# Modulation steps in the middle of wide token products, and q and k of a neighbourhood attention in 256 columns

## The chip, the cores and the metric

The kernel runs on one core of one Trainium2 chip. The metric is the time of one launch on the device in microseconds (us), the median of a few runs.

## The reference, cut to what matters

Two transformer blocks stand one behind the other, 256 tokens of x and 256 tokens of a context, 1024 features, all in float32. The first has two layers: modulation, a projection (`w_in`), differential attention, a short convolution and a Fourier mix, a projection back (`w_out`), layer norm, and an MLP of width 4096 with a squared ReLU. The second has an even layer (latent attention and a convolution) and an odd layer (RWKV with a decay, and a neighbourhood attention), each followed by 16 experts. What the change touches is this:

```python
mod_x = silu(c) @ w_mod[l] + b_mod[l]            # 6 * 1024 columns, for x and for ctx
sh1, sc1, g1, sh2, sc2, g2 = split(mod_x, 6)
px = (x * (1 + sc1) + sh1) @ w_in[l]
x = layer_norm(ALPHA * x + g1 * (mix_x @ w_out[l]))
x = layer_norm(ALPHA * x + g2 * (relu((x * (1 + sc2) + sh2) @ w_up[l]) ** 2 @ w_down[l]))
...
u = h @ od_w_in; uc = hc @ od_w_in               # odd layer: 1920 RWKV columns, then q, k, v
q, k = rms_norm(q by head), rms_norm(k by head)  # 8 heads of 64; q of x alone, k of x and ctx
```

## The kernel before

The program is laid out in the order of the blocks, and a scheduler puts each engine's instructions in a fixed order at build time: an instruction goes as early as its inputs, buffers and its rank in the program allow, by the scheduler's own estimate of times. On the chip each engine then runs its list in order. Buffers of one name are handed out in program order from a small pool: two PSUM banks "ps", two "pS", one "pt", two "pd", one "pm" (`BANKS`, L572).

**Products.** A float32 product is done as three: each operand is split into a high part (ScalarE cast, L347) and the rest (VectorE subtraction, L350), and high x high, high x low and low x high are summed in PSUM (L327 issues all of them). `by_features` (L398) takes weights of 256 columns as one load of 1 MB and gives features x tokens. `by_tokens` (L422) takes 512 columns as two loads of 1 MB, each 512 rows deep, and gives tokens x 512 columns: it opens one bank per block of 128 tokens, goes through four pairs of 128 rows, splits a pair (L383, three buffers each for the parts "wh" and "wl"), and multiplies it into every bank, so all banks are complete at the end. The banks are taken in turn from `WIDE` (L571). It is called for V (L756) and the output projection (L880) of the first block's mixer, for the second MLP matrix (L947), for the latent attention (L1186, L1200), the even layer's output (L1311) and the odd layer's q, k and v (L1693, L1698).

**The weight ring.** All loads of weights take a slot of 1 MB (`raw`, L366): three in one pool and one in another, used by every fourth load. They are issued on SyncE's queue (SP).

**Modulation steps.** Each of the four modulations (first block's layers, second block's layers) is a generator of 24 steps, eight for each of three banks of 2048 columns (`mods_steps`, L482). A step is one load of 1 MB through the ring (L532) and four small products into the bank "pm"; the eighth step of a bank copies it out (L502), transposes it through "ps" and adds the bias. `fill(n)` (L535) advances the front generator by n steps, up to a limit that the stages raise. Every call of `by_features` and of `by_tokens` ends with `fill(self.rate)`, the rate being 1. Before the output projection `need(m, 1)` (L866) and at the start of the MLP `need(m, 2)` (L902) force what is missing of a bank. Then `fill(BF[2 * l])` (L907) hands out four more, of the next modulation. In the first layer's mixer nine products come before the output projection (k twice, q twice, V, four others), and 16 steps, two banks, must be done by the MLP; in the second layer's mixer two steps come before the nine products. The second block's first modulation may hand out 18 steps (`NF`) until its own layer begins.

**The odd layer's input stage** (`odd_in`, L1628). RWKV's columns go by features. Then `lengths` (the norm of k in RWKV), the transposes of V (L1681), and `low_rank` (L1685: eight products of decays and rates) each use "ps" banks in turn. Then `NO` (L1554) lists k (tokens of x and context, four blocks), q (two blocks) and v (four blocks). k and q are copied out into tiles "nz" of two token blocks x 512 columns (two buffers), normed by head (`head_norm`, L990: per 512 columns a square into a "ps" bank by ScalarE and a sum by VectorE; then a chain of eleven small VectorE instructions for the root, and one multiplication), transposed 128 x 128 through "ps" and copied to the tiles "nk" and "nq" (L1708). The pools of the stage close after it, and the RWKV core follows.

Of the kernel before, what the change touches and what calls it, by code (L numbers as in the profile page):

```python
# [74 lines left out]
def every(n, w=256):  # L75
    return [(c, w) for c in range(0, n, w)]
# [9 lines left out]
def lay_out(inp):  # L86
# [10 lines left out]
    for name, blocks, rows in (  # L97
            ("ev_w_in_2", [(1184, 256), (672, 256), (1440, 256), (928, 256), (384, 256), (640, 32), (0, 256), (256, 128)],
             None),
            ("ev_w_out_2", every(1024, 512), 512), ("mla_w_uq_2", [(0, 512), (512, 256)], None),  # L100
            ("mla_w_ukv_2", every(1024, 512), None), ("od_w_in_2", every(1792) + [(1792, 128)], None),
            ("od_w_in_2", [(1920 + c, 512) for c in range(0, 1536, 512)], 512)):
        packs.setdefault(name, Packed())
        packs[name].add(g[name][0], blocks, rows)
    packs["od_w_out_2"] = Packed()
# [143 lines left out]
class Kernel:  # L249
# [148 lines left out]
    def by_features(self, src, ah, al, n, evac, halves=False, raw=None, le=None):  # L398
# [20 lines left out]
                self.fill(self.between)  # L419
        self.fill(self.rate)  # L420

    def by_tokens(self, srcs, ah, al, tbs, evac, ks=None):  # L422


        srcs = sorted(srcs, key=lambda z: ks.index(z[1])) if ks else srcs
        raws = [(self.load(z), k0) for z, k0 in srcs]
        ps = {tb: self.psum(self.bank()) for tb in tbs}
        pairs = [(raw, k0, i) for raw, k0 in raws for i in range(0, raw.shape[1], 2)]
        if ks:
            pairs.sort(key=lambda z: ks.index(z[1] + z[2]))  # L430
        for n, (raw, k0, i) in enumerate(pairs):
            kn, w = min(2, raw.shape[1] - i), raw.shape[2]
            wh, wl = self.parts(raw[:, i:i + kn])
            for tb in tbs:
                ts, out = slice(tb * 128, (tb + 1) * 128), ps[tb][:, :w]
                for j in range(kn):
                    h, l = ah[k0 + i + j][:, ts], al[k0 + i + j][:, ts]
                    end = n == len(pairs) - 1 and j == kn - 1
                    self.mm(out, h, wh[:, j], n + j == 0, False)
                    self.mm(out, h, wl[:, j], False, False)  # L440
                    self.mm(out, l, wh[:, j], False, end)
                if n == len(pairs) - 1:
                    evac(tb, out)
        self.fill(self.rate)

    def halves(self, w, c0, *where, first=0):
# [1125 lines left out]
class Odd(Moe):  # L1572
# [55 lines left out]
    def odd_in(self, m, od):  # L1628
# [3 lines left out]
        with self.dense():  # L1632
# [58 lines left out]
            for c0, n, dT in NO:  # L1691
                if dT is None:
# [1 line left out]
                                   lambda tb, ps: nc.scalar.copy(self.nv[:, tb], ps))  # L1694
                    continue
                dT = self.nkT if n == 4 else self.nqT
                zs = [tmp.tile([128, 2, 512], F32, name="nz", bufs=2) for _ in range(n // 2)]
                self.by_tokens(self.halves(a["od_w_in_2"], c0), ahs, als, range(n),  # L1698
                               lambda tb, ps: nc.scalar.copy(zs[tb // 2][:, tb % 2], ps))
                for tp, z in enumerate(zs):  # L1700
                    self.head_norm(z.rearrange("p t (h d) -> p (t h) d", h=8), 64)
                    for i in range(0, 4, 2):
                        ps = self.psum()
                        for i2 in range(2):
                            for tb in range(2):
                                self.transpose(ps[:, i2 * 256 + tb * 128:i2 * 256 + (tb + 1) * 128],
                                               z[:, tb, (i + i2) * 128:(i + i2 + 1) * 128])
                        nc.scalar.activation(dT[:, i:i + 2, tp * 256:(tp + 1) * 256],  # L1708
                                             ps.rearrange("p (i t) -> p i t", i=2), AF.Copy, scale=gain if n == 2 else 1.0)

    def lengths(self):

# [482 lines left out]
```

## Time and profile before

| what | value |
|---|---|
| median of three runs | 2853.8 us (2849.46 to 2855.07) |
| the profiled execution | 2856.6 us, of which its span 2854.8 us |
| TensorE (PE) busy | 2577.0 us |
| VectorE (DVE), ScalarE (ACT), GpSimd (POOL) busy | 1183.4, 770.8, 300.0 us |
| DMA over the span | 683.40 MB, mean 239 GB/s |
| first block and even layer, experts 1, odd layer, experts 2 | about 0 to 1400, 1400 to 1880, 1880 to 2390, 2390 to 2855 us |

All times within the profile are counted from the start of the span. A row of the timeline has the start, the duration, engine, line, operation, "tile written <- tiles read", shapes and count; in square brackets the engine's idle time before it and what ended that. A row of the slices of time has for each engine the busy time and, in brackets, the number of instructions. PEclk is the granted share of TensorE's full clock. Matmuls overlap, so the time of one is read from the distance of neighbours or from a run of many.

### The profile page before, as it was taken

What the parts mean: (1) busy time and instruction counts of PE and PEld (TensorE: products, weight loads), DVE (VectorE), ACT (ScalarE), POOL (GpSimd) and SP (SyncE); (2) the same over time, 40 slices, a digit from 0 to 9 for tenths busy, and PEclk for the clock granted to TensorE, in tenths of its full rate; (3) what the DMA queues carried; (4) which work ended last, traced back from release to release, by engine and by line L of the source; (5) the groups of instructions that cost most, each with busy time, mean ns of one, the idle gap of its engine ahead of it and who ended that gap; (6) DMA issues with size and microseconds to landing.
All of it is one profiled execution on the core that took longest, in us unless ns stands there. A gap on an engine that the chain in (4) does not pass through costs nothing.

```text
span 2854.8 us, 34268 instructions
## 1 busy us (share of the span) xinstructions
PE 2577.0 (90%) x13719; PEld 1563.0 (55%) x13719; DVE 1183.4 (41%) x2226; ACT 770.8 (27%) x1395; POOL 300.0 (11%) x361
## 2 busy tenths in 40 slices
PE   7998899997998998989799999989896997888888
PEld 4666688885765796757543333357544684222121
DVE  3365633346456467997401111155359362000000
ACT  3342322222333343366410000033442432000000
POOL 0001400004002003300100000000033130000000
PEclk9999999998999999999899999989898798999999
DMA  7335522223447764242599999952185558999998
GB/s 303 132 133 185 199 89 104 90 102 135 150 161 284 258 213 178 69 166 97 219 395 419 420 420 420 420 205 101 34 239 132 142 167 339 421 421 422 421 422 351
DMA packets 147215, 683.40 MB, mean 239 GB/s; under 512 B 38384, under 2 KB 51568, under 8 KB 71920
## 3 DMA queue, kind: packets, MB, share of 16 engines
q1 hardware_dynamic: 140800, 664.32, 60.6%
q10 hardware_dynamic: 6256, 16.90, 1.8%
q8 instruction: 108, 1.77, 0.3%
q14 instruction: 51, 0.42, 0.0%
HBM read 667.73 MB, written 11.60 MB: 238 GB/s over the span
## 4 chain that ended last, share of the span: by engine, by line
PE 54%; DMA 23%; DVE 8%; issue 2%; ACT 2%; POOL 0%; SPq 0%; DVEq 0%; POOLq 0%; ACTq 0%
DMA w<-in_moe_w 21%; PE pd L327 19%; PE pS L327 12%; PE pu L327 6%; PE pt L327 5%; PE ps L327 3%; PE pg L327 2%; PE pm L327 2%; DVE al L364 1%; PE pt L451 1%; PE ps L451 1%; PE pO L327 1%; DVE fs L1940 1%; PE py L327 1%; DVE co L1123 1%
## 5 line engine op out<-in xcount | busy, mean ns | idle before, releaser
L327 PE MATMUL pu<-w,xs 128*64 128x512 f32 (+1 forms) x2024 | 503.7, 599 | 41.4 <-DMA w<-in_moe_w 40.6
L350 DVE TENSOR_TENSOR wl<-w,wh 128x1024 fp32r<-128x1024 f32 x229 | 285.3, 1248 | 365.9 <-ACT wh L347 360.1
L347 ACT CAST wh<-w 128x1024 fp32r<-128x1024 f32 x250 | 259.8, 1043 | 609.9 <-PE pd L327 294.3
L327 PEld LDWEIGHTS pu<-w,xs 128*64 128x64 f32 (+1 forms) x2024 | 147.2, 123 | 374.7 <-issue 260.5
L327 PE MATMUL pd<-w,hidT 128*64 128x512 f32 (+1 forms) x1024 | 259.5, 598 | 30.3 <-DMA w<-in_moe_w 30.2
L327 PE MATMUL pd<-ah,wh 128*128 128x512 f32 (+2 forms) x656 | 233.5, 361 | 9.3 <-ACT wh L347 5.0
L327 PE MATMUL pd<-al,wh 128*128 128x512 f32 (+2 forms) x656 | 232.4, 356 | 6.7 <-DVE al L364 6.7
L327 PE MATMUL pd<-ah,wl 128*128 128x512 f32 (+1 forms) x648 | 227.5, 352 | 0.0
L1524 ACT ACTIVATE hid<-pu 128x512 f32<-128x512 f32 x24 | 14.2, 598 | 676.3 <-PE pu L327 676.3
L327 PEld LDWEIGHTS pd<-w,hidT 128*64 128x64 f32 (+1 forms) x1024 | 76.6, 122 | 198.3 <-issue 114.8
L1525 DVE TENSOR_TENSOR hid<-hid,pu 128x512 f32<-128x512 f32 x24 | 16.4, 688 | 396.9 <-PE pu L327 356.7
L327 PEld LDWEIGHTS pd<-ah,wh 128*128 128x128 f32 (+1 forms) x656 | 128.0, 197 | 46.5 <-issue 18.4
L327 PE MATMUL pm<-w,sil 128*32 128x512 f32 x640 | 108.5, 692 | 43.3 <-DMA w<-in_w_mod 31.0
L1534 DVE TENSOR_TENSOR ys<-pd,g 128x512 f32<-128x512 f32 x24 | 16.6, 692 | 315.1 <-PE pd L327 314.9
L327 PEld LDWEIGHTS pd<-al,wh 128*128 128x128 f32 (+1 forms) x656 | 128.4, 196 | 30.5 <-issue 8.3
L327 PEld LDWEIGHTS pd<-ah,wl 128*128 128x128 f32 x648 | 126.8, 196 | 20.3 <-issue 5.2
L1544 DVE TENSOR_TENSOR X<-X,ps 128x512 f32<-128x512 f32 x80 | 55.0, 688 | 128.1 <-PE ps L327 128.1
L1123 DVE SCALAR_TENSOR_TENSOR co<-cv,cols,co 128x512 f32<-128x512 f32 x120 | 100.9, 866 | 0.4
L327 PE MATMUL pS<-al,wh 128*128 128x256 f32 (+1 forms) x264 | 89.5, 340 | 4.2 <-DVE al L364 4.2
L327 PE MATMUL pS<-ah,wh 128*128 128x256 f32 (+1 forms) x264 | 89.3, 339 | 3.7 <-DVE tf L359 3.2
L327 PE MATMUL pS<-ah,wl 128*128 128x256 f32 (+1 forms) x264 | 88.6, 336 | 0.0
L327 PE MATMUL ps<-ys,gt 128*128 128x512 f32 x160 | 83.3, 629 | 0.6 <-DVE X L1544 0.6
(589 smaller groups left out, 4424.9 us busy)
## 6 DMA issues: line engine op xcount, KB each, us to landing
w<-in_moe_w SPq DMA_DIRECT2D x381, 1024.0 KB, 19.8
w<-in_w_mod SPq DMA_DIRECT2D x48, 1024.0 KB, 6.3
w<-in_w_up SPq DMA_DIRECT2D x32, 1024.0 KB, 4.8
w<-in_w_down SPq DMA_DIRECT2D x32, 1024.0 KB, 4.8
w<-in_ada_w SPq DMA_DIRECT2D x32, 1024.0 KB, 5.7
w<-in_w_in SPq DMA_DIRECT2D x20, 1024.0 KB, 4.8
mw<-in_ada_w SPq DMA_DIRECT2D x64, 256.0 KB, 3.5
w<-in_od_w_in SPq DMA_DIRECT2D x13, 1024.0 KB, 4.9
```

What stands on the lines that cost most here:

```text
L327: ins = self.nc.tensor.matmul(out, lhsT, rhs, start=start, stop=stop, skip_group_check=True)
L347: nc.scalar.copy(h, src)
L350: (le or nc.vector).tensor_tensor(l, src, h.bitcast(F32), OP.subtract)
L364: nc.vector.tensor_tensor(l, t, h.bitcast(F32), OP.subtract)
L451: ins = self.nc.tensor.transpose(out, in_, self.ident[:rows, :rows])
L1123: nc.vector.scalar_tensor_tensor(y, CV[:, f, :, t:t + T], self.col(f"dw{t}", f), y, OP.mult, OP.add)
L1524: nc.scalar.activation(hid[:, cs], up["moe_w1_2"][c], AF.Silu)
L1525: nc.vector.tensor_tensor(hid[:, cs], hid[:, cs], up["moe_w3_2"][c], OP.mult)
L1534: nc.vector.tensor_tensor(ys[:, cs], down[c], gate[:, cs], OP.mult)
L1544: nc.vector.tensor_tensor(self.X[tb][:, cs], self.X[tb][:, cs], ps, OP.add)
L1940: nc.vector.tensor_tensor(t, LM[:, s, tr, None].to_broadcast([128, nt_, nj]), X[:, s, None, jr].to_broadcast([128, nt_, nj]), OP.mult)
```

## The change

In `by_tokens` a call of `fill(self.rate)` is added after half of the pairs, where there are two or more; the one at the end stays. q and k of the neighbourhood attention are packed as four blocks of 1024 rows x 256 columns in place of two of 512 columns. A new function `by_pairs` loads such a block (1 MB), splits it in two parts, and multiplies it for two token blocks at a time into one bank, so that a bank is complete before the next is begun. The tile "nz" now holds all token blocks of 256 columns (four heads), still with two buffers, and norm, transposes and copies go by these column halves: two norms for k and two for q, where there were two for k (by token halves) and one for q. v is as before.

```diff
-("mla_w_ukv_2", every(1024, 512), None), ("od_w_in_2", every(1792) + [(1792, 128)], None),
-("od_w_in_2", [(1920 + c, 512) for c in range(0, 1536, 512)], 512)):
+("mla_w_ukv_2", every(1024, 512), None), ("od_w_in_2", every(1792) + [(1792, 128)] + [(1920 + c, 256) for c in range(0, 1024, 256)], None),
+("od_w_in_2", [(2944, 512)], 512)):
...
+    def by_pairs(self, src, ah, al, tbs, evac, ks=None):
+
+        raw = self.load(src)
+        kt, w = raw.shape[1], raw.shape[2]
+        ws = [self.parts(raw[:, k0:min(k0 + 4, kt)]) for k0 in range(0, kt, 4)]
+        for tp in tbs:
+            ps = self.psum(self.bank())
+            for i in range(2):
+                ts = slice((tp * 2 + i) * 128, (tp * 2 + i + 1) * 128)
+                out = ps[:, i * w:(i + 1) * w]
+                for n, k in enumerate(ks or range(kt)):
+                    h, l = ah[k][:, ts], al[k][:, ts]
+                    wh, wl = (z[:, k % 4] for z in ws[k // 4])
+                    self.mm(out, h, wh, n == 0 and i == 0, False)
+                    self.mm(out, h, wl, False, False)
+                    self.mm(out, l, wh, False, n == kt - 1)
+            evac(tp, ps[:, :2 * w].rearrange("p (a b) -> p a b", a=2))
+        self.fill(self.rate)
+
...
                 if n == len(pairs) - 1:
                     evac(tb, out)
+            if n == len(pairs) // 2 - 1:
+                self.fill(self.rate)
         self.fill(self.rate)
...
-                zs = [tmp.tile([128, 2, 512], F32, name="nz", bufs=2) for _ in range(n // 2)]
-                self.by_tokens(self.halves(a["od_w_in_2"], c0), ahs, als, range(n),
-                               lambda tb, ps: nc.scalar.copy(zs[tb // 2][:, tb % 2], ps))
-                for tp, z in enumerate(zs):
-                    self.head_norm(z.rearrange("p t (h d) -> p (t h) d", h=8), 64)
-                    for i in range(0, 4, 2):
+                for j in range(2):
+                    z = tmp.tile([128, 4, 256], F32, name="nz", bufs=2)[:, :n]
+                    self.by_pairs(W(c0 + j * 256), ahs, als, range(n // 2),
+                                   lambda tp, ps: nc.scalar.copy(z[:, tp * 2:tp * 2 + 2], ps))
+                    self.head_norm(z.rearrange("p t (h d) -> p (t h) d", h=4), 64)
+                    for i in range(2):
                         ps = self.psum()
-                        for i2 in range(2):
-                            for tb in range(2):
-                                self.transpose(ps[:, i2 * 256 + tb * 128:i2 * 256 + (tb + 1) * 128],
-                                               z[:, tb, (i + i2) * 128:(i + i2 + 1) * 128])
-                        nc.scalar.activation(dT[:, i:i + 2, tp * 256:(tp + 1) * 256],
-                                             ps.rearrange("p (i t) -> p i t", i=2), AF.Copy, scale=gain if n == 2 else 1.0)
+                        for tb in range(n):
+                            self.transpose(ps[:, tb * 128:(tb + 1) * 128], z[:, tb, i * 128:(i + 1) * 128])
+                        nc.scalar.activation(dT[:, 2 * j + i], ps[:, :n * 128], AF.Copy, scale=gain if n == 2 else 1.0)
```

## Rows read from the trace of the kernel before

**Rows 1.** The page: busy time, the chain that ended last, step loads (us to landing).
```profile
PE 2577.0 (90%) x13719; PEld 1563.0 (55%) x13719; DVE 1183.4 (41%) x2226; ACT 770.8 (27%) x1395; POOL 300.0 (11%) x361
...
PE 54%; DMA 23%; DVE 8%; issue 2%; ACT 2%; POOL 0%; SPq 0%; DVEq 0%; POOLq 0%; ACTq 0%
...
w<-in_w_mod SPq DMA_DIRECT2D x48, 1024.0 KB, 6.3
```

**Rows 2.** Slices of 10 us in the first layer's mixer.
```profile
220.00:230.00 10.00, 10.00 (x68) 8.99 (x67) 4.51 (x16) 3.27 (x7) 1.82 (x4) 1.00 0.00 0
...
250.00:260.00 10.00, 4.82 (x26) 1.43 (x28) 2.09 (x4) 0.00 (x0) 0.00 (x0) 0.84 0.89 360
```

**Rows 3.** Timeline of TensorE, first layer's output product.
```profile
252.17 1.07 PE L327 MATMUL pm<-w,sil 128*32 128x512 f32 x8 [0.96 <-DMA w<-in_w_mod]
257.46 3.22 PE L327 MATMUL pm<-w,sil 128*32 128x512 f32 x16 [4.22 <-DMA w<-in_w_mod]
```

**Rows 4.** Timeline of TensorE, second layer, ahead of the output product.
```profile
823.70 1.11 PE L451 MATMUL ps<-cst,tf 128*128 128x128 f32 x4 [4.38 <-DVE tf L794]
```

**Rows 5.** Timeline of TensorE, second layer's output product and start of the MLP.
```profile
850.82 1.06 PE L327 MATMUL pm<-w,sil 128*32 128x512 f32 x6
...
857.03 2.77 PE L327 MATMUL pm<-w,sil 128*32 128x512 f32 x20
...
862.11 1.07 PE L327 MATMUL pm<-w,sil 128*32 128x512 f32 x8 [0.97 <-ACT sil L490]
...
871.78 0.39 PE L327 MATMUL pt<-ah,wh 128*128 128x256 f32 x1 [1.19 <-ACT wh L347]
...
879.31 0.58 PE L327 MATMUL pt<-ah,wl 128*128 128x256 f32 x1 [7.03 <-DVE wl L350]
```

**Rows 6.** Timeline of SP's queue there.
```profile
863.24 0.33 SPq L380 DMA_DIRECT2D w<-in_w_up  x1
```

**Rows 7.** Timelines of VectorE and GpSimd there.
```profile
869.98 0.76 DVE L364 TENSOR_TENSOR al<-tf,ah 128x256 fp32r<-128x256 f32 x2
...
870.77 2.45 DVE L364 TENSOR_TENSOR al<-tf,ah 128x256 fp32r<-128x256 f32 x1
...
876.35 2.90 DVE L350 TENSOR_TENSOR wl<-w,wh 128x1024 fp32r<-128x1024 f32 x1
...
870.57 4.86 POOL L625 TENSOR_TENSOR X<-X,gb 128x1024 f32<-128x1024 f32 x2 [4.99 <-PE ps L451]
875.39 6.09 POOL L626 TENSOR_TENSOR X<-X,gb 128x1024 f32<-128x1024 f32 x2
```

**Rows 8.** Chain that ended last, odd layer's input stage (start, us, what, count).
```profile
1953.25 5.44 PE pS L327 x24
...
1964.44 2.88 PE pS L327 x24
...
2047.26 6.64 PE pS L327 x18
```

**Rows 9.** Slice of 10 us at the end of the odd layer's input stage.
```profile
2035.00:2045.00 10.00, 3.83 (x14) 2.16 (x13) 4.53 (x14) 2.51 (x5) 0.00 (x0) 0.84 0.00 0
```

**Rows 10.** Timelines of ScalarE, TensorE and VectorE in that stage.
```profile
2003.64 0.59 ACT L1699 COPY nz<-pd 128x512 f32<-128x512 f32 x1 [0.77 <-PE pd L327]
...
2035.71 1.98 PE L327 MATMUL ps<-lwa,low 64*128 64x512 f32 x4
2043.86 1.94 PE L451 MATMUL ps<-cst,nz 128*128 128x128 f32 x8 [6.17 <-DVE nz L1003]
...
2057.61 1.03 PE L451 MATMUL ps<-cst,nz 128*128 128x128 f32 x8
...
2059.22 0.61 ACT L999 ACTIVATE ps<-nz 128x512 f32<-128x512 f32 x1
...
2063.89 1.22 DVE L1003 TENSOR_TENSOR nz<-nz,rstd 128x1024 f32<-128x1024 f32 x1
...
2067.24 0.69 ACT L1708 ACTIVATE nq<-ps,nag 128x512 f32<-128x512 f32 x1 [0.17 <-PE ps L451]
```

## The prediction

> **What bounds the kernel now.** I read the page first: TensorE is busy 90% of the span, and the chain that ended last is 54% TensorE and 23% DMA [rows 1]. So the kernel is a TensorE chain with one DMA stretch in it (the expert weights), and a change pays where TensorE sits idle, or where an instruction that blocks its in-order queue goes. I then looked at the two places that the diff touches, in slices of 10 us and instruction by instruction.
>
> The first place is the modulation steps. A step is one load of 1 MB and four small products, 1.06 us of TensorE [rows 5]. In the first mixer the DMA engines moved nothing from 220 to 230 us, and from 250 to 260 TensorE was busy for less than half while they ran at 0.89 [rows 2]. What TensorE waited for there were step loads: 0.96 and 4.22 us, and the two steps behind the second wait took 3.22 us [rows 3]. The loads come in a burst because a ring of four slots holds all weights, and the steps that nobody handed out earlier are forced at the end of the mixer, behind the four loads of the output product.
>
> The same holds in the second layer, with another price. Its forced steps run until 859.8, the next modulation's first step runs at 862.11, and only when that has given its slot back, at 863.2, is the first load of the MLP issued, at 863.24 [rows 5, 6]. TensorE then waits 1.19 us for the high part of that load's split and 7.03 us for its low part [rows 5], which VectorE does at 876.35 in 2.90 us [rows 7], while GpSimd runs.
>
> The second place is the last part of the RWKV/neighbourhood input stage. TensorE is full until 2037.7; in the next ten microseconds it is busy for 3.83 [rows 9]. From there to 2067.9 the head norms of k (two) and q (one) follow each other, since all of them, and before them the decay and rate products, take the two "ps" banks in program order. The core of the RWKV part starts when the last copy is out [rows 10].
>
> **The change part by part.** (1) *Steps handed out in the middle of wide products.* Counting in the code: in the first layer V now hands out two steps and each of the two output products two, so two steps are forced where five were; in the second layer none where three were. The total of steps, of their loads on SP's queue and of their TensorE time is the same, so the gain is only in waits.
>
> First layer: at most the two waits, 5.2 us, and the slow part of 3.22 against two steps at 1.06, 1.1 us: 6.3 us. One of the forced steps keeps a slot that the last half of the output weights gives back late; a step load takes 6.3 us to land at the median [rows 1], and it is placed on TensorE's queue as now. I leave 2.3 us of waiting to it and take **-4**; bounds 0 and -6.3.
>
> Second layer: two steps inside the output product, of 1.06 us like the one at 850.82 [rows 5], can run earlier, in the idle 4.38 us before 823.70 [rows 4]: -2.1, bounds 0 and -2.1. Then the MLP's first load: its slot no longer waits for forced steps, so the split can be done before GpSimd's pass begins at 870.57 [rows 7]. That takes away 1.19 us [rows 5], and from VectorE's queue one split of 2.90 us; what is late next are the low parts "al", of which one took 2.45 us in that stretch and two together 0.76 us just before [rows 7]. By rows -4.1, bounds 0 and -8.2 (both waits whole).
>
> The Trainium skill has a rule against this: in "SBUF — State Buffer", section "Who interferes with whom", a VectorE instruction with two SBUF inputs and a GpSimd instruction that reads SBUF exclude each other, and the later one waits for the end of the other. The trace agrees in kind (2.45 us against 0.38). By that rule alone the last "al" would still come at the end of GpSimd's work, and the term would be about -1.3.
>
> GpSimd's passes stay where they are and last to 881.5 or so, so some of the low parts remain slow; I take **-3** for the load and **-2** for the two steps.
>
> New in both mixers is that the second output product's loads follow the release of the first's in the ring, where some followed a step's: they have half a product, 5 us and more, against a landing of about that [rows 1], and behind them on SP's queue stand step loads only. Late, they would hold a split on ScalarE and the products behind it: 0, bounds 0 and +2.
>
> In the second layer's MLP the 18 allowed steps go out earlier by a few products; TensorE is full there and the DMA engines are not, so 0, and if a load came late its wait would stand there (about 1 us each). In the other calls of the token products the limits stop every step, or the product is a single pair: 0.
>
> (2) *k and q by 256 columns.* Product time: 144 products of 512 columns become 288 of 256. 24 of the first kind take 5.44 us and 24 of the second 2.88 [rows 8], 0.227 and 0.120 us each: 288 x 0.120 - 144 x 0.227 = **+1.9 us**, on a full TensorE, so it moves the start of the tail; bounds 0 (if the tail's idle time absorbs it) and +1.9. Loads of q and k on SP's queue: four of 1 MB before and after; splits: eight of 1024 elements before and after, on ScalarE and VectorE. A part is now needed within half a product; the products of r in 256 columns ran at 2.88 us [rows 8] with the same rhythm of splits, so 0. Evacuations of k and q: six of 512 elements, as before.
>
> The tail: k still has two norms of 16 heads, by column half in place of token half, each with two squares and eight transposes: no change. q has two norms of 8 heads in place of one of 16. The one took from 2059.22 to 2067.93, 8.7 us [rows 10]. A half drops one of two squares (0.6), half of the multiplication of 1.22 us (0.6) and half of the transposes (1.94 us when slow, 1.0) [rows 10]: 6.5. The second half's square needs a "ps" bank that the first half's first copy frees, one half copy or 0.4 us ahead of its end: 6.5 + 6.1 = 12.6 against 8.7, **+3.9**. Bounds: a whole extra norm, +8.7; and below, -3.5, worked out with the rivals. I take the middle value, since it is made of the rows of the very norm that is cut in two. The work that could cover it, what is left of v's products after 2037.7, lies between the norms already and is done before q's norm ends.
>
> Sum: -4 -2 -3 +1.9 +3.9 = -3.2. Against the profiled execution of 2856.6 us (span 2854.8 and 1.8 around it) this is 2853.4. The median of the three runs, 2853.8, is 2.8 below that execution, so I forecast 2850.5. A later start of the expert stages moves with it: their loads are released by the stages before them.
>
> **The rivals.** *The tail of q decides (slower).* Place: the input stage of the odd layer, 2037 to 2068. If the q halves run one after the other without any overlap, and the extra product time counts in full, it costs 8.7 + 1.9 = 10.6; if at the same time the steps are forced into the same in-order waits as now, only 2 of the 9 us are won: +8.6, 2862. It decides from the point where the tail grows by more than the first part wins, about 9 us. For it: every bank of the tail is handed over in program order, and TensorE has nothing to do there. Against it: a half norm has less of everything but the root.
>
> *The shorter units keep the tail going (faster).* After the idle stretch the granted clock was lower (a mean of 0.84 in its ten microseconds [rows 9], so part of it at 1.2 in place of 2.4 GHz): eight transposes took 1.94 us at 2043.86 and 1.03 at 2057.61 [rows 10], and 18 products of v took 6.64 us from 2047.26 [rows 8], where 18 x 0.227 is 4.1. If k's first columns, complete after half of the product, let the norms fill that stretch, 2.5 us of products and two times 0.9 us of transposes come back, and half of the idle 6.17 us ahead of the first transposes [rows 10]: 7.4. The second part is then -1.6 in place of +5.8; with the first part at -9 the time is 2843. Against it: the norms wait for the banks of the decay products, not for k, whose copies were out at 2004.2 [rows 10].
>
> *The first part does nothing.* Steps are placed by readiness, not by the place in the program, so handing them out earlier may leave the same last loads in the same place; and while GpSimd runs the activations' low parts are as slow (2.45 us [rows 7]), so the 7.03 us may only change its name from "wl" to "al". Then -2, and with +3 to +6 of the second part 2855 to 2858.
>
> **How the numbers follow.** Forecast (2845 to 2856): 0.45. Faster rival: 0.22. Nothing from the first part: 0.14. Slower rival: 0.19. What a measurement of this kernel can tell from no change is 0.2%, 5.7 us: faster is below 2848.1, slower above 2859.5. Of the forecast 0.18 lies below 2848.1 and 0.27 within; the faster rival is all faster; the third case is within, but for 0.02; the slower rival lies above but for 0.01. So faster 0.40, same 0.40, slower 0.20. The range for 8 in 10: from 2839 (the first part at its bounds of -6.3, -2.1 and -8.2 with the second near +2) to 2861; the rest is the upper half of the slower rival and the lower end of the faster one. The forecast's own range is 2845 to 2856.
>
> **What would show it right or wrong.** Right: no wait for a step load between 245 and 265 over 3 us; the first load of the second layer's MLP issued ahead of 858, and the 7.03 us wait below 4; the stage slices after the neighbourhood products with a stretch of low TensorE time some 5 us longer, four root chains of VectorE in it in place of three. Wrong: if the tail is shorter than 30 us, the step that failed is that the norms wait for the banks of the decay products; if the waits for the modulation loads stand as they are, it is that the burst comes from steps not handed out.

## The result, and the profile after

The changed kernel took 2825.05 us (median of four runs, 2821.36 to 2829.69) where the kernel before took 2854.44 beside it: a ratio of 0.9896 [0.987, 0.9922], 29.4 us faster. The forecast was 2850.5 and the lower end of its range 2839. The direction was right, the size was not, and of the two parts one had the wrong sign. The profiled execution took 2825.67 us, of which the span is 2823.9.

The page after, beside [rows 1]: TensorE is busy 13.0 us less with 144 more instructions; 9 us of that lie in one stretch where the granted clock was 0.90 in place of 0.75 (see the end of this section). The step loads land after 5.0 us where they took 6.3.

```profile
PE 2564.0 (91%) x13863; PEld 1565.1 (55%) x13863; DVE 1184.7 (42%) x2238; ACT 769.4 (27%) x1397; POOL 301.4 (11%) x361
...
w<-in_w_mod SPq DMA_DIRECT2D x48, 1024.0 KB, 5.0
```

Slices of 10 us after. The first answers to [rows 2]: from 250 to 260 TensorE is full where it had 4.82, at a DMA share of 0.18. The second answers to [rows 9]: at the end of the odd layer's input stage TensorE still has a slice that is nearly empty, 2.97 against 3.83, but it is the only one. In the whole stage TensorE's idle time, added up from the gaps in front of its instructions, went from 13.9 to 7.0 us.

```profile
250.00:260.00 10.00, 10.00 (x46) 8.21 (x45) 7.43 (x14) 2.10 (x2) 1.94 (x4) 1.00 0.18 48
...
2035.00:2045.00 10.00, 2.97 (x14) 2.06 (x13) 4.24 (x16) 4.28 (x8) 1.26 (x1) 0.65 0.32 105
```

Timeline of TensorE, SP, VectorE and GpSimd after, second layer. No wait for a step load is left in the first layer's output product [rows 3]. In the second layer the idle 4.38 us of [rows 4] has a step in it, behind a wait of 2.40. The 7.03 us of [rows 5] are gone: the MLP's first load goes out at 843.82, not 863.24 [rows 6]. A wait of 7.19 us for a step load of the next modulation has come in at 857.8, and the waits for low parts of the activations are 1.18 and 1.76 us. Three of those parts took 7.15 us beside GpSimd, whose pass begins at 873.07 and not at 870.57 [rows 7]. Between 720 and 940 (times of the kernel before) TensorE's idle time went from 20.2 to 13.8 us in all.

```profile
820.84 1.06 PE L327 MATMUL pm<-w,sil 128*32 128x512 f32 x8 [2.40 <-DMA w<-in_w_mod]
...
855.04 2.78 PE L327 MATMUL pm<-w,sil 128*32 128x512 f32 x24
...
865.02 1.94 PE L327 MATMUL pm<-w,sil 128*32 128x512 f32 x8 [7.19 <-DMA w<-in_ada_w]
...
878.33 0.39 PE L327 MATMUL pt<-al,wh 128*128 128x256 f32 x1 [1.18 <-DVE al L364]
...
880.83 0.58 PE L327 MATMUL pt<-al,wh 128*128 128x256 f32 x1 [1.76 <-DVE al L364]
...
843.82 0.33 SPq L380 DMA_DIRECT2D w<-in_w_up  x1
...
876.13 7.15 DVE L364 TENSOR_TENSOR al<-tf,ah 128x256 fp32r<-128x256 f32 x3
...
873.07 4.92 POOL L646 TENSOR_TENSOR X<-X,gb 128x1024 f32<-128x1024 f32 x2 [10.10 <-PE ps L472]
```

The chain of waits after, odd layer's input stage (start, us, what, count), beside [rows 8]: the products of 512 and 256 columns cost what they did, and 18 products of v take 4.08 us where 18 took 6.64.

```profile
1935.67 5.44 PE pS L327 x24
...
1943.99 2.88 PE pd L327 x24
...
2024.91 4.08 PE pS L327 x18
```

Where the 30.9 us of span came from, read by setting the same instruction of both profiles side by side:

| piece of work, by its start or end in the profile before | shift after (us) |
|---|---|
| until 110 | 0 |
| until the first layer's MLP runs without gaps (338.7, after 333.1) | -5.6 |
| first layer's MLP, until 720 | +2.2 |
| second layer's mixer and the start of its MLP, until that runs (940) | -13.1 in all |
| end of its MLP's first part (1045) | -17.7 in all |
| even layer and experts, until the odd input stage's second gate (tile sgs, copied out of bank pS; 1948.6, after 1931.0) | -17.6 in all |
| odd input stage, until the RWKV core's first product (2068.49, after 2044.08) | -24.4 in all |
| RWKV core until 2209.7 | +4.6 |
| 2209.7 to 2270.6 | -9.1 |
| the rest | -2.0 |

The -9.1 us at the end is no work of the change: the idle time there is the same (7.1 and 7.0 us), the busy time went from 53.8 to 44.8, and the granted clock of the stretch was 0.75 before and 0.90 after. A second execution of the changed kernel did not have it; more on it in the last section.

### The profile page after: what moved, and what is told of

It reads as the page before. It is cut to its first block, busy times and chain, and to the rows that moved or that the text cites. A ratio compares the mean times of both kernels' runs of the same rounds, so it can differ in the third digit from the quotient of the medians.

```text
span 2823.9 us, 34571 instructions
## 1 busy us (share of the span) xinstructions
PE 2564.0 (91%) x13863; PEld 1565.1 (55%) x13863; DVE 1184.7 (42%) x2238; ACT 769.4 (27%) x1397; POOL 301.4 (11%) x361
## 4 chain that ended last, share of the span: by engine, by line
PE 55%; DMA 23%; DVE 7%; issue 2%; ACT 2%; SPq 0%; POOL 0%; ACTq 0%; DVEq 0%; POOLq 0%
DMA w<-in_moe_w 21%; PE pd L327 20%; PE pS L327 12%; PE pu L327 7%; PE pt L327 6%; PE ps L327 4%; PE pg L327 2%; PE pm L327 2%; DMA w<-in_ada_w 1%; DVE al L364 1%; PE ps L472 1%; PE pt L472 1%; PE py L327 1%; PE pO L327 1%; DVE fs L1958 1%
## 5 line engine op out<-in xcount | busy, mean ns | idle before, releaser
L1545 ACT ACTIVATE hid<-pu 128x512 f32<-128x512 f32 x24 | 14.2, 597 | 676.3 <-PE pu L327 676.3
L327 PEld LDWEIGHTS pd<-ah,wh 128*128 128x128 f32 (+1 forms) x656 | 127.1, 195 | 42.2 <-issue 15.2
L327 PE MATMUL pS<-al,wh 128*128 128x256 f32 (+1 forms) x264 | 89.5, 340 | 4.9 <-DVE al L364 4.9
```

Of the source, the lines that this page charges most:

```text
L327: ins = self.nc.tensor.matmul(out, lhsT, rhs, start=start, stop=stop, skip_group_check=True)
L1545: nc.scalar.activation(hid[:, cs], up["moe_w1_2"][c], AF.Silu)
```

## Experiments

**The two parts, each alone.** The steps alone are the kernel before with the two added lines of `by_tokens`; the blocks alone are the kernel after without them.

```diff
             if n == len(pairs) // 2 - 1:
                 self.fill(self.rate)
```

> Only the first part: the extra hand-out in the middle of the token products; k and q of the neighbourhood attention as before. Theory: the two parts are separate, and this one gives what the trace of the changed kernel shows until the odd layer begins, 17.6 us (5.6 in the first layer, the rest in the second): 2835 to 2839 us, and the odd layer's input stage is as long as before (110.9 us between the evacuation of the gates and the first evacuation of the RWKV core). Rival: the 9 us that the changed kernel wins between 2209 and 2271 us hang on when that stretch begins, so they come with this part too: 2826 to 2830.

> Only the second part: k and q by 256 columns, no hand-out in the middle. Theory: the input stage of the odd layer is 6.8 us shorter, of which 3.4 go back in a wait for modulation loads that now come late, and the stretch between 2209 and 2271 us is a matter of the granted clock: 2842 to 2851 us. Rival: that stretch's 9 us belong to this part whenever it runs: 2840 to 2843, with the same 52 us in that stretch.

> The kernel before once more, for a second profile. Theory: the stretch from 2209 to 2271 us, 60.9 us long with 22 us at a granted clock of 0.50, depends on when a clock reading falls, so it is 3 us or more off 60.9 in another execution. Rival: it is a property of the order of the instructions and is within 1 us of 60.9.

> The changed kernel once more, for a second profile. Theory: the same stretch, 51.8 us in the first profile, varies by 3 us or more from one execution to the next. Rival: within 1 us of 51.8.

Measured, all beside each other: the steps alone 2831.36 us (0.9936 [0.9923, 0.9948]), the blocks alone 2849.27 (1.0002 [0.999, 1.0014]), the kernel before 2851.95 (1.0008 [0.9997, 1.0018]), the kernel after 2824.32 (0.9909 [0.9895, 0.9923]). By these ratios the steps carry most of it, some 18 us, a little more than was expected of them, and the blocks by themselves are worth nothing, yet with the steps they bring 7.7 us (0.9936 to 0.9909, two intervals that just touch). The profile of the blocks alone explains half of this: its input stage is as short as after (111.6 us, before 119.9), and its RWKV core starts 7.5 us early. That execution was the lowest of its twelve (2842.69, up to 2864.14); the median shows nothing of those 8 us. Behind the input stage the scheduler has laid the lists of the RWKV core in another order than before; that this is where and why they are lost was not shown.

The two second profiles settle the stretch from 2209.7 on: between the same two instructions (2210.82 to 2264.43 in the first profile before) it took 53.6 and 47.5 us in the kernel before, 44.8 and 53.0 in the kernel after. It differs by 6 and 8 us between executions of one kernel. The steps alone have a profile too:

> The first part alone once more, for its profile alone (the run before left one in which the chip ran at a much lower clock). Theory: the same rows as in the changed kernel until the odd layer (waits for step loads gone in the first layer, first load of the second MLP issued before 850, steps of that MLP in one piece each) and the odd layer's input stage as before, 119 to 120 us from its first evacuation of the gates to the first product of the RWKV core. Rival: the input stage is shorter here too, since it only depends on when it begins.

Its input stage is 119.9 us as before, and the shift ahead of it is -6.2 in the first layer, -18.75 at 1045 and -15.3 at the odd layer. (This execution took 2841.32 us as a whole, 10 more than the median of the steps alone.) So the input stage belongs to the blocks and all the earlier gain to the steps.

**Which of the middle hand-outs works.** `by_tokens` gets a parameter `mid=False`, the added line becomes `if mid and n == ...`, and in the kernel before one call alone passes `mid=True`: the output product (`w_out`), the second MLP matrix (`w_down`), or V.

```diff
-self.by_tokens(self.halves(a["w_out"], j * 512, l), ahs, als, TB[nv], evac, WK)
+self.by_tokens(self.halves(a["w_out"], j * 512, l), ahs, als, TB[nv], evac, WK, mid=True)
```

> The extra hand-out only in the four output products of the mixers (two in each layer), all else as before. Theory: the forced steps are what costs, so this gives most of the first part's 18 us: 8 to 14 us, the first layer's two waits and the 7 us wait of the second layer's MLP among them. Rival: the steps inside the MLP's products decide, and this gives 2 to 5 us.

> The extra hand-out only in the second product of the MLP (eight products in each layer). Theory: only the pieces of steps in the second layer's MLP come together again, about 4 us (five pieces of 0.98 us with nothing else won): 2 to 6 us. Rival: the MLP is where the first part works: 10 us or more.

> The extra hand-out only in the product of V (one in each layer). Theory: one forced step less in each mixer, 1 to 4 us. Rival: nothing at all, within 1 us, since the steps behind it are still forced.

Measured: `w_out` 2847.77 (0.9986 [0.9973, 0.9999]), `w_down` 2849.34 (0.9984 [0.9973, 0.9995]), V 2834.26 (0.9952 [0.9934, 0.9969]). Two of the three forecasts missed: `w_out` was to bring 8 to 14 us and V 1 to 4. By the profiles, V's alone takes 11.5 us off the first layer; 5 of these are gone by the middle of the second layer (some 2 of them also between two profiles of the kernel before, the rest is open), and the start of the second MLP gives 8.8 (a shift of -6.45, then -15.2). `w_out`'s takes away both step waits of [rows 3], which the prediction had named as the cause, and the first layer becomes 3.9 us *longer*: TensorE waits at the same place for an evacuation (timeline of TensorE, VectorE and ScalarE's queue, `w_out` alone).

```profile
259.45 0.79 PE L327 MATMUL pS<-wh,ah 128*128 128x512 f32 x1 [5.54 <-DVE tf L877]
...
258.70 0.69 DVE L877 TENSOR_TENSOR tf<-pS,qk 128x512 f32<-128x512 f32 x1 [6.27 <-DMA qk<-modrm]
...
249.17 0.83 ACTq L569 DMA_DIRECT2D qk<-modrm  x2
```

What ends that wait is `qk`, the gate row g1, by which every output block is multiplied as it leaves its bank. The row is made by the sixteenth modulation step: transposed through the "ps" banks, written to memory, and read back to all partitions. In the kernel before (timeline of TensorE, ScalarE's queue and VectorE) these instructions stand in the following order, and the evacuation waits 8.30 us for the read:

```profile
239.14 0.60 PE L451 MATMUL ps<-cst,modrow 128*128 128x128 f32 x4
...
242.13 0.34 ACTq L520 DMA_DIRECT2D modrm<-modrow  x1
...
247.40 0.84 ACTq L567 DMA_DIRECT2D qk<-modrm  x2
...
257.91 0.69 DVE L875 TENSOR_TENSOR tf<-pS,qk 128x512 f32<-128x512 f32 x1 [8.30 <-DMA qk<-modrm]
```

After, the same instructions:

```profile
233.49 0.60 PE L472 MATMUL ps<-cst,modrow 128*128 128x128 f32 x4
...
238.19 0.34 ACTq L541 DMA_DIRECT2D modrm<-modrow  x1
...
242.98 0.83 ACTq L588 DMA_DIRECT2D qk<-modrm  x2
...
248.30 0.69 DVE L896 TENSOR_TENSOR tf<-pS,qk 128x512 f32<-128x512 f32 x1
```

The banks of the product were full; the row was late. In the program the sixteenth step stands behind the last attention heads in the kernel before, so its row takes its turn of "ps" behind theirs; one hand-out more at V or earlier puts it ahead of them.

`w_down`'s run shows another gain that was not foreseen. Timeline of TensorE, second layer's MLP, in the kernel before: one step, split by the order of the list into pieces of two, four and two instructions (each of its four products is two in the trace), costs about 1 us for each piece.

```profile
919.81 1.05 PE L327 MATMUL pm<-w,sil 128*32 128x512 f32 x2
...
923.74 1.05 PE L327 MATMUL pm<-w,sil 128*32 128x512 f32 x4
...
927.22 1.04 PE L327 MATMUL pm<-w,sil 128*32 128x512 f32 x2
```

With `w_down`'s middle hand-out:

```profile
920.88 1.07 PE L327 MATMUL pm<-w,sil 128*32 128x512 f32 x8
...
927.54 1.07 PE L327 MATMUL pm<-w,sil 128*32 128x512 f32 x8
```

From 940 to 1045, where TensorE has no idle time in either kernel, eight steps stood in 11 pieces before, and seven stand in seven pieces here; that stretch is 4.6 us shorter, about 1 us for each of the four pieces.

V's run shows what became of the 7.03 us of [rows 5]. Timeline of VectorE and GpSimd, V alone: both low parts of the MLP's first load are split, at 1.22 us each, before GpSimd's pass begins; before, the second fell into the pass and took 2.90 [rows 7].

```profile
863.89 1.22 DVE L350 TENSOR_TENSOR wl<-w,wh 128x1024 fp32r<-128x1024 f32 x1
...
865.48 1.22 DVE L350 TENSOR_TENSOR wl<-w,wh 128x1024 fp32r<-128x1024 f32 x1
...
868.51 5.73 POOL L627 TENSOR_TENSOR X<-X,gb 128x1024 f32<-128x1024 f32 x2 [9.82 <-DVE al L364]
```

**Is it the gate row?** Three kernels, each the kernel before with one edit. The first reads the first layer's gate row from an input that is there from the start (a layer norm's gain), so that the gate is left out of the result in that layer; the second hands out in V's middle in the first layer alone; the third leaves V as it is and hands out one step more behind the first product of the first layer.

```diff
-self.row_in(m["row"][0][v], G[:, v])
+self.row_in(a["ln1_g"][l] if l == 0 else m["row"][0][v], G[:, v])
```

```diff
+            if l == j == 0:
+                self.fill()
```

> The kernel before, but in the first layer the output product's evacuation is multiplied by rows read straight from an input (a layer norm's gain) in place of the gate row that the modulation step writes out and reads back; so the gate is left out of the result, and all work stays. Theory: TensorE stood still from 253.24 to 257.46 because the banks of the output product wait for the gate row (VectorE waited 8.30 us for it and began at 257.91), not for step loads: 6 to 11 us faster, all of it between 238 and 300 us. Rival (the prediction's): the step loads hold TensorE, so the waits of 0.96 and 4.22 us stay and the gain is under 2 us.

> The kernel before with one extra hand-out in all: in the middle of V's product of the first layer. Theory: this one moves the sixteenth step, and with it the gate row, ahead of the last attention heads' turns at the two banks, so the output product ends some 10 us earlier and the first layer is 9 to 12 us shorter; the second layer's MLP keeps its 7 us wait. Rival: the first layer's gain in the run with both V products came from the ring's turn (which slot a load takes) and needs nothing of the gate: then the gate row is as late as before, and the layer still shorter.

> The kernel before with one extra hand-out in all, but after the first product of the first layer (k's first columns), so that the loads take other slots of the ring than with V's. Theory: any one step more before the ninth product does the same: gate row at about 240 us, output product 8 to 11 us earlier. Rival: it is V's place in the ring that counts: less than 4 us.

Measured: 2855.78 (1.001 [0.9997, 1.0023]), 2836.87 (0.9945 [0.9929, 0.9962]) and 2844.97 (0.9969 [0.9956, 0.9982]). In the last two the first layer is 9.5 and 9.3 us shorter by the profile, and the evacuation starts at 242.74 and 242.94, where it started at 257.91. So in the first layer it is not V's place that matters but that the sixteenth step is out before the last heads. (The two medians differ by 8 us all the same, with shifts of -13.0 and -14.2 in the profiles at 1045; what sets them apart lies behind that and is open.) Timeline of the one-step kernel:

```profile
237.37 0.83 ACTq L567 DMA_DIRECT2D qk<-modrm  x2
...
242.94 0.69 DVE L877 TENSOR_TENSOR tf<-pS,qk 128x512 f32<-128x512 f32 x1 [0.39 <-DMA qk<-modrm]
```

The first kernel is a miss that taught more. Its evacuation starts at 236.47 and its output product ends at 269.96, 8.7 us ahead of before, and at 338 all of it is given back and 3.8 us more. Its timeline (TensorE, SP, VectorE, GpSimd) at the start of the first MLP: the third load of `w_up` goes out only at 298.63, and two weight parts are split in 4.04 us beside GpSimd. In the kernel before, with the same steps still to do there, that load went out at 288.65 (the last row, timeline of SP).

```profile
297.52 0.58 PE L327 MATMUL pS<-ah,wl 128*128 128x256 f32 x1 [4.94 <-DVE wl L350]
...
298.63 0.33 SPq L380 DMA_DIRECT2D w<-in_w_up  x1
...
294.56 4.04 DVE L350 TENSOR_TENSOR wl<-w,wh 128x1024 fp32r<-128x1024 f32 x2
...
286.37 5.05 POOL L625 TENSOR_TENSOR X<-X,gb 128x1024 f32<-128x1024 f32 x2 [4.52 <-ACT ah L363]
...
288.65 0.33 SPq L380 DMA_DIRECT2D w<-in_w_up  x1
```

An early row alone is therefore worth nothing here (+3.8), and taking away the waits for step loads with the row still late is worth nothing either (`w_out` alone, +3.9); the kernels with one step more ahead of the last heads have the row early and one step fewer left for later, and gain 9. Why the loads of `w_up` come later when the row alone is early was not shown.

**The input stage.** Two forms of the blocks, in the kernel after. The first keeps 256 columns, but opens all four banks of a block at once as `by_tokens` does, all complete at the end. The second has k as after, and q in 512 columns with one norm as before.

```diff
-self.by_pairs(W(c0 + j * 256), ahs, als, range(n // 2),
-               lambda tp, ps: nc.scalar.copy(z[:, tp * 2:tp * 2 + 2], ps))
+self.by_tokens([(W(c0 + j * 256), 0)], ahs, als, range(n),
+               lambda tb, ps: nc.scalar.copy(z[:, tb], ps), step=4)
```

> The changed kernel, with k and q by 256 columns through the old routine: parts of 1024 elements, all banks open from the first half of the rows to the last, all complete at the end. Theory: the input stage is shorter because products of 256 columns let the chain of small steps through sooner, whatever the banks: 111 to 114 us from the first evacuation of the gates to the first product of the RWKV core, like the changed kernel. Rival: what counts is that a bank is complete after half the product, so norms start earlier: 117 to 120 us, like before.

> The changed kernel, with q as before (512 columns, one norm) and k alone by 256 columns. Theory: the chain of small steps runs beside k's products, which come first, so k alone gives the short stage: 111 to 114 us. Rival: q's halves give it, since q's norm is the last: 117 us or more.

Measured: 2838.47 (0.9929 [0.9905, 0.9954]) and 2828.40 (0.9904 [0.9884, 0.9924]). The first of these is slower than the kernel after as a whole by more than its input stage is; where it loses the rest is open. By the starts of three instructions in each profile, in us from the second gate of the stage (the row of the table above):

| kernel | V copied | last decay/rate activation | RWKV core's first product |
|---|---|---|---|
| before, first and second profile | 56.4, 56.4 | 89.5, 89.5 | 119.9, 119.1 |
| steps alone | 56.4 | 89.5 | 119.9 |
| blocks alone | 48.4 | 75.7 | 111.6 |
| after, first and second profile | 49.9, 48.4 | 77.2, 75.7 | 113.0, 111.6 |
| all banks to the end | 50.6 | 77.4 | 114.8 |
| k alone | 49.9 | 81.3 | 113.7 |

k's blocks alone win 6.2 us of the 7 to 8, and 256 columns with all banks open win 5.1. So neither an early complete bank nor q is what matters most. What does is seen in the middle columns: the chain of `lengths`, the transposes of V and `low_rank` ends some 12 to 14 us sooner (8 with k alone). Two links of `lengths` in a row (timeline of TensorE), before and after:

```profile
1973.01 2.74 PE L327 MATMUL ps<-tf,cst 128*8 128x512 f32 x6
...
1979.77 1.02 PE L327 MATMUL ps<-tf,cst 128*8 128x512 f32 x2
```

```profile
1955.43 2.74 PE L327 MATMUL ps<-tf,cst 128*8 128x512 f32 x6
...
1960.33 1.02 PE L327 MATMUL ps<-tf,cst 128*8 128x512 f32 x2
```

6.76 us against 4.90, with 17 products between the two in both. The other links stand unevenly, but over the whole chain, from these first links to the last products of `low_rank` (2035.71, after 2007.08), the trace has 198 products of 512 columns between the links before and 260 of 256 columns after: at the 0.227 and 0.120 us of [rows 8], 44.9 and 31.2 us. The norms of k still wait for the "ps" banks of the decay products, as the prediction said: after, k's first columns were copied out by 1973.8 and its second by 1994.1, but its first square (2005.68) starts right behind the activation at 2004.96, which frees a bank. Timeline of ScalarE and TensorE after, beside [rows 10]:

```profile
2004.96 0.69 ACT L1769 ACTIVATE av<-ps,cols 128x512 f32<-128x512 f32 x1 [0.36 <-PE ps L327]
2005.68 0.60 ACT L1020 ACTIVATE ps<-nz 128x512 f32<-128x512 f32 x1
...
2031.81 0.64 ACT L1020 ACTIVATE ps<-nz 128x512 f32<-128x512 f32 x1
...
2042.62 0.90 ACT L1727 ACTIVATE nq<-ps,nag 128x256 f32<-128x256 f32 x2 [4.58 <-PE ps L472]
...
2044.08 0.58 PE L327 MATMUL py<-tri,sgs 128*128 128x256 f32 x1 [1.07 <-ACT tri L1809]
...
2055.91 3.16 PE L327 MATMUL pd<-mw,sil 128*32 128x512 f32 x6 [3.43 <-DMA mw<-in_ada_w]
```

But then v's products are still to come and fill TensorE until v is done, at 2035.3; only what is left then of q's two half norms (2031.81 to 2043.52) stands alone. The idle time of the stage shows it. TensorE's waits in it before, beside the 6.17 us of [rows 10] (timeline of TensorE, its last wait of 1.28 left out), and after (its last, of 1.07 us, is in the row of 2044.08):

```profile
2047.26 0.79 PE L327 MATMUL pS<-wh,ah 128*128 128x512 f32 x1 [1.46 <-ACT nz L1699]
...
2065.26 1.94 PE L451 MATMUL ps<-cst,nz 128*128 128x128 f32 x8 [4.99 <-DVE nz L1003]
```

```profile
2036.26 0.63 PE L472 MATMUL ps<-cst,nz 128*128 128x128 f32 x4 [0.94 <-DVE nz L1024]
...
2041.92 1.09 PE L472 MATMUL ps<-cst,nz 128*128 128x128 f32 x4 [5.03 <-DVE nz L1024]
```

The waits for k's norm, 6.17 and 1.46 us, are gone, and q's is 5.97 in place of 4.99: 6.9 us less in all, the gain of the stage. The last row of the timeline before these is a part that was given back: the loads "mw" of the next modulation are released by the end of the stage and are late by 3.43 us in that profile.

**A better one.** In the first layer `w_out`'s middle hand-out costs some 4 us, as its own run showed (3.9). Four kernels go on from the one after: no middle hand-out in any `w_out` (V and `w_down` alone), none in the first layer's, and the latter with q as before; the last one, and the kernel after, once more beside each other.

```diff
+    def by_tokens(self, srcs, ah, al, tbs, evac, ks=None, mid=True):
...
-self.by_tokens(self.halves(a["w_out"], j * 512, l), ahs, als, TB[nv], evac, WK)
+self.by_tokens(self.halves(a["w_out"], j * 512, l), ahs, als, TB[nv], evac, WK, mid=l == 1)
```

> The changed kernel without the extra hand-out in the four output products. Theory: the hand-out there costs the first layer some 5 us and brings nothing that the others do not bring: 3 to 7 us below the changed kernel, 2818 to 2822. Rival: the parts do not add, and this is within 2 us of the changed kernel.

> The changed kernel without the extra hand-out in the first layer's output product alone. Theory: the first layer gains 11 in place of 6 us, the second as in the changed kernel: 4 to 6 us less up to the odd layer, and 2817 to 2822 us if the RWKV part is in the same order as in the changed kernel; if the scheduler orders it anew, up to 15 us are lost there, as in the run without any hand-out in the output products. Rival: the parts do not add before the odd layer either: within 2 us of the changed kernel there.

> The same with k alone by 256 columns, q as before. Theory: 4 to 6 us less than the run with k alone up to the odd layer, an input stage of 113 to 114 us, and 2820 to 2825 us if the RWKV part keeps its order. Rival: as in the run before this one.

> The changed kernel once more, on the chip of the next run. Theory: as before, 0.989 to 0.991 of the kernel before.

> The kernel without the hand-out in the first layer's output product and with k alone by 256 columns, beside the changed kernel. Theory: the 4 us that the first layer keeps show in the total: a ratio 0.001 to 0.003 below the changed kernel's. Rival: what it wins in the first layer is lost in the RWKV part's order: the same ratio within 0.0005.

| kernel | median (us) | ratio to before |
|---|---|---|
| V and `w_down` with blocks | 2840.41 | 0.9955 [0.9934, 0.9977] |
| none in the first `w_out` | 2823.05 | 0.9904 [0.9885, 0.9922] |
| the same, q as before | 2818.95 | 0.9878 [0.9859, 0.9898] |
| after, beside the next | 2825.59 | 0.9913 [0.9892, 0.9935] |
| the same, q as before, again | 2818.51 | 0.9879 [0.9863, 0.9895] |

By the profiles the first layer of the second and third is 10.1 and 9.2 us shorter than before, where in three profiles of the kernel after it is 5.6 to 7.7, and their RWKV core starts 32.7 and 30.8 us early, where after it is 24.4 to 28.5. The version without the first layer's hand-out in `w_out`, with q in 512 columns, is the fastest found: 7.1 us below the kernel after on the same chip, with intervals that just touch. The first row is a warning, and its forecast, 2818 to 2822 us, missed: it reaches the RWKV core 26.4 us early and by its ratio is only 12.8 us faster. In its profile the core's scan takes 157.2 us, where it takes 140 to 147 in all the others. VectorE's list there is in another order than before; but so it is in others that are not slow there, the fastest kernel among them, so the order by itself does not explain it, and the cause stays open. It stands beside the blocks alone, 7.5 us early at the core and with no gain at the end.

## Why the prediction was wrong, step by step

**First layer: -4 forecast, -5.6 measured, for the wrong reason.** "The gain is only in waits" for step loads failed as a step. Taking those waits away alone made the layer 3.9 us longer; what ended last there was the gate row, whose read landed at 257.89, behind both of them. The rows of that were in the trace of before, on VectorE, and I had read TensorE's waits alone. An early row alone gave nothing either. One step handed out early, which moves both, gives -9.3 to -11.5, and the hand-outs in `w_out`, which I had counted as the gain, take some 4 of it back.

**Second layer, mixer and start of the MLP: -2 and -3 forecast, -9.7 measured (a shift of -3.4 at 720, -13.1 at 940; -10.9 between the two second profiles).** The mechanism was right: the load left 19 us earlier, its split was done ahead of GpSimd, and the 7.03 us were gone. What was mis-sized is the term of -3: I thought that more than half of the two waits would move to the activations' low parts. These are slow, 7.15 us for three where two took 0.76 without GpSimd [rows 7]. The Trainium skill has a rule for it ("SBUF — State Buffer", "Who interferes with whom": a VectorE instruction with two SBUF inputs and GpSimd's reads exclude each other), and the trace agrees in kind. But products already ran between them, and of their waits 3.2 us stood on TensorE. The wait of 7.19 us for a step load, which I had put at "about 1 us each", is in the -9.7 already: of TensorE's idle time 6.4 us are gone between 720 and 940, and the rest is busy time, six steps from 880 to 940 in six pieces in place of nine among it.

**"In the second layer's MLP ... so 0": -4.6.** The pieces from 940 to 1045 went from 11 to 7, at about 1 us a piece. That a step's place in the list decides its price, and not only its time, I had not seen, though [rows 5] had pieces of 6, 8 and 20.

**Blocks: +5.8 forecast, -7 to -8 in the input stage.** The two costs were right: the stage's products cost what [rows 8] say, and q's two half norms took 11.7 us against 12.6. The step that failed is the one that the sum never names: that the chain of small steps ahead of the norms keeps its times. It ended 12 to 14 us sooner, since its links stand between products, and these took half as long each; so the norms of k fell under the products of v, and 6.9 us of waits on TensorE were gone. The nearest rival, the shorter units that keep the tail going, had the end of it right (v's 18 products at 4.08 us, its 4.1) and the cause wrong. My sign for that, a tail shorter than 30 us, came true and would have blamed the wrong step: the norms do wait for the decay products' banks.

**The sum.** First layer -5.6, its MLP +2.2, the second layer -14.3 and the input stage -6.8 make the -24.4 at the core's start (in round numbers). Beside runs of the kernel before, 25 to 30 us were measured. In the first two profiles the rest adds -6.5, with -9.1 in the stretch of the higher granted clock; in the second two the core starts 28.4 us early and the span is 22.8 shorter, so there the rest takes 5.6 back. So behind the core's start no gain of the change is shown, and how much of the 25 to 30 us is clock in a given run is open.

## What to carry to other kernels

Where an engine waits for a load, look also at what the *next* instruction on each other engine waits for at that moment: of two late things, taking away the one that the idle engine names can gain nothing. In an in-order list a chain of small steps is as slow as the work between its links is long; here narrower products shortened it although their sum was larger. And where a scheduler lays the order anew, a part is worth what the whole run says: two edits of 18 and 0 us made 25 to 30 together.

## What the hardware showed that I had not expected

*The granted clock stays low with TensorE busy.* In the RWKV scan of the kernel before TensorE is busy for 5.15 to 6.15 of 10 us in the slices from 2168.5 to 2208.5. Behind it, after a wait of some 6 us, it is busy without a gap, and the granted clock is at 0.50 (1.2 GHz) for 20 us in some executions and back at 1.00 (2.4 GHz) sooner in others. Slices of the kernel before:

```profile
2230.00:2240.00 10.00, 10.00 (x108) 6.67 (x108) 5.28 (x12) 5.50 (x13) 0.00 (x0) 0.50 0.11 27
2240.00:2250.00 10.00, 10.00 (x96) 6.73 (x94) 2.49 (x7) 2.78 (x6) 0.00 (x0) 0.50 0.61 199
```

The kernel after, first and second profile, as one slice each between the same two instructions (the first product of keys and queries and the first product `pg<-U,BK`):

```profile
2190.05:2234.81 44.76, 37.80 (x593) 28.47 (x589) 21.61 (x48) 19.89 (x41) 1.80 (x1) 0.89 0.49 125
```

```profile
2183.29:2236.28 52.99, 47.33 (x592) 34.66 (x588) 21.47 (x47) 20.23 (x41) 1.80 (x1) 0.71 0.42 106
```

The same work is busy for 37.80 us at a mean clock of 0.89 and for 47.33 at 0.71: 9.5 us that come and go with one and the same kernel. In the kernel before the same stretch was busy for 46.54 us at 0.71 and, in its second profile, for 42.80 at 0.78. A single profile can't tell a gain of that size. The Trainium skill ("TensorE: Matmul & The Clock Gate", "Part 1: The HAM clock gate") has the clock rise once TensorE has been busy. The slices from 2230 to 2250 do not agree: by the profile TensorE was busy for 10.00 us in the first, and in the second the clock was still at 0.50.

*A step's products cost the same in pieces.* Two instructions took 1.04 us and all eight of a step 1.07, and where 11 pieces became 7 the stretch was 4.6 us shorter.

*A row's way through memory.* From the issue of the gate row's write to the landing of the second of its two copies: 242.13 to 257.89, 15.8 us (5.3 until the reads were issued), while the loads of the ring were under way (a DMA share of 0.89 from 250 to 260 [rows 2]).
